# Forming half of the low parts of the first MLP product's weights with ScalarE and an accumulating DMA

## The chip, the core and the metric

The kernel runs on one core of one Trainium2 chip. The metric is the device time in microseconds of one execution. Each time is from a run of the whole program; the median of three runs is compared.

## The reference, cut to what matters

A decoder trunk of two layers on 256 tokens of width 2048, all in float32. Layer 0 has a mixer of a gated short convolution and differential attention, layer 1 has forgetting attention; each layer ends with a dense MLP whose hidden width is 8192:

```
def _sqrelu_mlp(h, w1, w2):
    return jnp.square(jax.nn.relu(h @ w1)) @ w2

for l in range(DEPTH):
    h = _rmsnorm(x, norm1_g[l])
    ...                                    # x = x + mixer(h)
    h = _rmsnorm(x, norm2_g[l])
    x = x + _sqrelu_mlp(h, mlp_w1[l], mlp_w2[l])
```

`mlp_w1` is 2 x 2048 x 8192 and `mlp_w2` 2 x 8192 x 2048. The weights of all products together are some 400 MB, read once, so the kernel is a stream of weights through 256 tokens.

## The kernel before

Every large product goes through `gemm(acts, w, c0)`, which makes 256 tokens x 512 columns in two PSUM tiles. To keep nearly float32 precision with matmuls on the narrower type float32r, each operand is split into a high part (the value rounded to float32r) and a low part (the rest, rounded too), and three products are added: high x high, high x low of the weights, low x high. The activations are split when they are made (`ActT`); the weights are split in `gemm`, as they arrive.

The weights come in raw tiles of 512 rows x 512 columns (1 MB), loaded by SP's DMA queue into a pool of three buffers (L135). Each raw tile is worked in two halves, h = 0 and 1. For a half tile ScalarE casts the raw values into the high part `wh` (L141), VectorE subtracts it from the raw values into the low part `wl` (L142), and TensorE does 12 matmuls: two token tiles, two k tiles, and the three products (L148 with `wh`, L149 with `wl`, L150 with `wh` and the low part of the activations). `wh` and `wl` have four buffers each. A buffer of `wh` is free again when the half tile that used it has gone through TensorE; a raw tile is free when both its halves are split.

`mlp` has four groups of hidden columns per layer. In each it does four products with w1 (L524), each followed by relu on ScalarE (L529), a multiplication on VectorE (L530) and transposes on TensorE (L514), and then four products with w2 (L538) over these 2048 hidden columns, added to the residual (L540). A product with w1 has 4 raw tiles, thus 8 half tiles; there are 2 x 16 such products.

The order of the instructions on each engine isn't that of the code. The kernel is written as a data flow over tile pools; when it is built, a scheduler puts each engine's instructions in an order of its own, by what it expects to be ready, and adds the waits. That order is then fixed: an engine's queue goes through it one by one, and an instruction that waits holds those behind it. The small work (attention, norms, transposes) is written as generators in `pending`, of which `step()` emits a stage after each half tile.

POOL has little to do: it makes masks at the start and adds the mask to the bias of layer 1's attention (L462).

Of the kernel before, what the change touches and what calls it, by code (L numbers as in the profile page):

```python
# [8 lines left out]
F32 = mybir.dt.float32  # L9
F32R = mybir.dt.float32r  # L10
# [16 lines left out]
def trunk_kernel(  # L27
# [20 lines left out]

    # ---------------------------------------------------------------- inputs
    xr = [resid.tile([P, 2, CW], F32, name=f"xr{n}") for n in range(NCH)]  # L50
# [9 lines left out]

    # per-channel vectors come as rows and are transposed: channels on partitions
    g1 = const.tile([P, 32], F32, name="g1")
# [10 lines left out]

    # ---------------------------------------------------------------- helpers
    pending = []

    def step():
        """Emit one more stage of the work that runs beside the large products."""
        while pending:
            try:  # L80
                next(pending[0])
                return True
            except StopIteration:
                pending.pop(0)
        return False
# [5 lines left out]
    def rsqrt(out_t, ss, inv_n, n):  # L91
        """out = (ss * inv_n + EPS) ** -0.5, one Newton step behind the tables."""
        v = small.tile([P, n], F32, name=f"rv{n}")
        nc.vector.tensor_scalar(v, ss, inv_n, EPS, ALU.mult, ALU.add)
        y = small.tile([P, n], F32, name=f"ry{n}")
        nc.scalar.activation(y, v, AF.Ln)
        nc.scalar.activation(y, y, AF.Exp, scale=-0.5)
        t = small.tile([P, n], F32, name=f"rt{n}")
        nc.vector.tensor_tensor(t, y, y, ALU.mult)
        nc.vector.scalar_tensor_tensor(t, t, -0.5, v, ALU.mult, ALU.mult)  # L100
        nc.vector.scalar_tensor_tensor(out_t, t, 1.5, y, ALU.add, ALU.mult)

    class ActT:
        """Transposed activations, four k tiles: high and low parts."""

# [6 lines left out]
        def split(self, sel, src, scalar, n):  # L112
            """hi/lo[sel] = parts of src * scalar; n: how many k tiles' worth it is."""
            hi, lo = self.hi[sel], self.lo[sel]
            if scalar is None:
                nc.scalar.copy(hi, src)  # L116
                nc.vector.tensor_tensor(lo, src, hi.bitcast(F32), ALU.subtract)  # L117
            else:
                nc.scalar.activation(hi, src, AF.Copy, scale=scalar)
                nc.vector.scalar_tensor_tensor(lo, src, scalar, hi.bitcast(F32), ALU.mult, ALU.subtract)  # L120
            self.left -= n

    def gemm(acts, w, c0, first=False):
        """acts @ w[:, c0:c0+512] -> two PSUM tiles (tokens x columns)."""
        acc = [accp.tile([P, CW], F32, name="acc") for _ in range(2)]
        total = 4 * len(acts)
        i = 0
        for ai, a in enumerate(acts):
            raw = wraw.tile([P, 4, CW], F32, name="raw")
            src = w[a.row:a.row + CW, c0:c0 + CW].rearrange("(k p) n -> p k n", p=P)  # L130
            if first and ai == 0:
                for h in range(2):
                    nc.sync.dma_start(raw[:, 2 * h:2 * h + 2, :], src[:, 2 * h:2 * h + 2, :])
            else:
                nc.sync.dma_start(raw, src)  # L135
            until(lambda: a.left <= 0)
            for h in range(2):
                wh = wspl.tile([P, 2, CW], F32R, name="wh")
                wl = wspl.tile([P, 2, CW], F32R, name="wl")
                rw = raw[:, 2 * h:2 * h + 2, :]  # L140
                nc.scalar.copy(wh, rw)  # L141
                nc.vector.tensor_tensor(wl, rw, wh.bitcast(F32), ALU.subtract)  # L142
                for t in range(2):
                    ts = slice(t * P, (t + 1) * P)
                    for j in range(2):
                        k = 2 * h + j
                        st, sp = i + j == 0, i + j == total - 1
                        nc.tensor.matmul(acc[t], a.hi[:, k, ts], wh[:, j, :], start=st, stop=False)  # L148
                        nc.tensor.matmul(acc[t], a.hi[:, k, ts], wl[:, j, :], start=False, stop=False)  # L149
                        nc.tensor.matmul(acc[t], a.lo[:, k, ts], wh[:, j, :], start=False, stop=sp)  # L150
                i += 2
                step()
        return acc

    class Norm:
        """Pre-RMSNorm of the residual: transposed x * g by chunk, and 1/rms by token."""

# [32 lines left out]
    def proj(nm, w, c0, name, first=False):  # L190
        """Rows of (norm(x) @ w)[:, c0:c0+512] in SBUF."""
        acc = gemm(nm.acts, w, c0, first)
        o = qkv.tile([P, 2, CW], F32, name=name)
        for t in range(2):
            nc.scalar.activation(o[:, t, :], acc[t], AF.Copy, scale=nm.r(t))
        return o

    # ---------------------------------------------------------------- setup
    # (emitted once the first loads are under way)
    lam_init = 0.8 - 0.6 * math.exp(-0.3 * 0)  # L200
# [10 lines left out]
    def setup():  # L211
# [14 lines left out]

        # causal masks: [first block | full block | diagonal block]
        nc.gpsimd.memset(mask, 0.0)
# [12 lines left out]
        nc.vector.tensor_copy(sv, ps[:, :NROW])  # L241
        # diff: q gain x k gain x scale; fox: the same; sub-norm gain x (1 - lambda_init)
        nc.vector.scalar_tensor_tensor(gains[:, 0:1], sv[:, 56:57], 64.0 ** -0.5, sv[:, 57:58], ALU.mult, ALU.mult)
        nc.vector.scalar_tensor_tensor(gains[:, 1:2], sv[:, 59:60], 128.0 ** -0.5, sv[:, 60:61], ALU.mult, ALU.mult)
        nc.vector.tensor_scalar(gains[:, 2:3], sv[:, 58:59], 1.0 - lam_init, None, ALU.mult)
        yield
        # -lambda on every partition
        lp = work.tile([P, 2, P], F32, name="y")[:, :, :64]
# [8 lines left out]
    def head_norm(tiles, hd):  # L257
        """RMS-normalise groups of hd columns of [P, 2, CW] tiles, in place, without gain."""
        g = CW // hd
# [33 lines left out]
    def prob_transposed(p):  # L293
        """[queries, (q0 k0 | q1 k0 | q1 k1)] -> the three blocks transposed."""
        ps = tpp.tile([P, CW], F32, name="tp")
        for b in range(3):
            nc.tensor.transpose(ps[:, b * P:(b + 1) * P], p[:, b * P:(b + 1) * P], ident)  # L297
        pT = work.tile([P, 3 * P], F32, name="pT")
        nc.scalar.copy(pT, ps[:, :3 * P])
        return pT  # L300

    # stages of four heads, staggered
    STAGES = [("T", 0), ("S", 0), ("T", 1), ("S", 1), ("P", 0), ("T", 2), ("A", 0), ("S", 2),
              ("P", 1), ("T", 3), ("A", 1), ("S", 3), ("P", 2), ("A", 2), ("P", 3), ("A", 3)]

    # ------------------------------------------------------- layer 0: mixers
    def diff_attention(q, k, v, a):
# [52 lines left out]
    def conv_mixer(c, u, b, half, a):  # L360
        """Gated causal convolution of 512 channels, channels on partitions."""
        for t in range(2):
# [24 lines left out]

    # ------------------------------------------------------- layer 1: mixer
    fc = const.tile([P, 2, 16], F32, name="fc")
    fcd = dram.tile([16, 2 * P], F32, name="fcd")  # L390

    def forget_gates(nm):
        """fc: cumulated log gates; fcd: their negative by head."""
        wv = gws[:, :KT * 32].rearrange("p (k n) -> p k n", n=32)
# [3 lines left out]
        yield  # L398
        # rows 0-15: high parts of w, rows 16-31: low parts; the other rows are not used
        acc = tpp.tile([P, CW], F32, name="tp")  # L400
# [26 lines left out]
        nc.vector.tensor_scalar(u, e, 1.0, None, ALU.add)  # L427
        # log1p(e) = ln(u) + (e - (u - 1)) / u
        nc.vector.scalar_tensor_tensor(d, u, -1.0, e, ALU.add, ALU.subtract)
# [67 lines left out]

    # ---------------------------------------------------------------- layers
    def out_proj(acts, w, nxt):
        """x += concat(acts) @ w; the last k block apart, as its input comes last."""  # L500
        for part in (acts[:-1], acts[-1:]):
            for n in range(NCH):
                acc = gemm(part, w, n * CW)
                for t in range(2):
                    nc.vector.tensor_tensor(xr[n][:, t, :], acc[t], xr[n][:, t, :], ALU.add)  # L505
                if len(part) == 1:
                    pending.append(nxt.chunk(n))

    def mlp(nm, l, nxt):
# [10 lines left out]
        for g in range(4):  # L520
            hT = []
            for n in range(4):
                c0 = (4 * g + n) * CW
                acc = gemm(nm.acts, mlp_w1[l], c0)  # L524
                a = ActT(c0)
                # relu(h)^2 without the 1/rms of each token, which follows behind w2
                r = [work.tile([P, CW], F32, name="junk") for _ in range(2)]
# [91 lines left out]
```

## Time and profile before

| | |
|---|---|
| runs | 2219.1, 2219.4, 2220.47 us; median 2219.4 |
| span of the profiled execution, first to last instruction | 2217.6 us (no time of its own is listed beside it; the runs lie 1.5 to 2.9 us above it) |
| TensorE matmul busy | 2207.0 us (100%) |
| VectorE busy | 1245.1 us (56%) |
| ScalarE busy | 1029.5 us (46%) |
| POOL busy | 13.7 us (1%) |
| DMA, mean | 186 GB/s, 412.02 MB |
| granted TensorE clock | 1.000, of 2.4 GHz |

An engine is busy while one of its instructions runs. Matmuls overlap: one has a duration of 390 ns, and they start about 227 ns apart (12 in 2.72 us). Idle time counts against an engine only where nothing else is in the way. "What ended it" names the instruction whose completion let the waiting one go.

### The profile page before, as it was taken

How to read it: one execution, taken by the hardware profiler on the slowest of the kernel's cores; microseconds unless marked ns; L12 is line 12 of the kernel's file. 1: busy time of each engine (PE TensorE's matmuls, PEld its weight loads, DVE VectorE, ACT ScalarE, POOL GpSimd, SP SyncE). 2: the span in 40 equal slices, each digit the busy share in tenths (PEclk: the TensorE clock that was granted, in tenths of full speed). 3: DMA queues.
4: the chain of work that ended last, by engine and by line, in shares of the span. 5: the costliest groups of instructions: out<-in, count | busy, mean ns of one | idle time of the engine just before them, and what ended most of it. 6: DMA issues, size and time to landing. Idle time of an engine off the chain costs nothing.

```text
span 2217.6 us, 25167 instructions
## 1 busy us (share of the span) xinstructions
PE 2207.0 (100%) x10100; PEld 1824.2 (82%) x10100; DVE 1245.1 (56%) x1480; ACT 1029.5 (46%) x1351; POOL 13.7 (1%) x17
## 2 busy tenths in 40 slices
PE   8999999999999999999999999999999999999999
PEld 7887888888888888888888888888888888888887
DVE  5666666655555555455556566666555555555554
ACT  6555444543443444344455555455434434443443
POOL 0000000000000000000000000000000000000000
PEclk9999999999999999999999999999999999999999
DMA  7555555555555555555555555555565555555564
GB/s 254 171 172 167 174 190 190 176 184 194 190 186 191 192 187 190 192 188 190 182 175 189 185 185 178 178 171 179 183 195 191 184 190 194 185 190 194 186 199 142
DMA packets 212470, 412.02 MB, mean 186 GB/s; under 512 B 9367, under 2 KB 13698, under 8 KB 212354
## 3 DMA queue, kind: packets, MB, share of 16 engines
q1 hardware_dynamic: 204496, 405.84, 56.2%
q10 hardware_dynamic: 7858, 4.58, 0.7%
q8 instruction: 79, 1.29, 0.2%
q14 instruction: 37, 0.30, 0.0%
HBM read 408.28 MB, written 2.11 MB: 185 GB/s over the span
## 4 chain that ended last, share of the span: by engine, by line
PE 99%; ACT 0%; DMA 0%; DVE 0%; SPq 0%; issue 0%
PE acc L148 32%; PE acc L150 32%; PE acc L149 32%; PE tp L514 1%; PE tp L169 1%; PE tp L285 0%; PE tp L297 0%; PE tp L473 0%; PE tp L493 0%; DMA xr<-in_x_dram 0%; PE tp L494 0%; PE tp L472 0%; PE tp L371 0%; PE tp L321 0%; PE tp L320 0%; PE tp L405 0%
## 5 line engine op out<-in xcount | busy, mean ns | idle before, releaser
L142 DVE TENSOR_TENSOR wl<-raw,wh 128x1024 fp32r<-128x1024 f32 x768 | 942.3, 1228 | 883.1 <-ACT wh L141 882.5
L141 ACT CAST wh<-raw 128x1024 fp32r<-128x1024 f32 x768 | 807.4, 1052 | 1081.3 <-PE acc L150 1039.2
L148 PE MATMUL acc<-wh,act_hi 128*128 128x512 f32 x3072 | 1219.2, 397 | 2.0 <-ACT wh L141 2.0
L150 PE MATMUL acc<-wh,act_lo 128*128 128x512 f32 x3072 | 1200.2, 391 | 0.0
L149 PE MATMUL acc<-wl,act_hi 128*128 128x512 f32 x3072 | 1198.5, 390 | 0.0
L150 PEld LDWEIGHTS acc<-wh,act_lo 128*128 128x128 f32 x3072 | 577.2, 188 | 122.8
L148 PEld LDWEIGHTS acc<-wh,act_hi 128*128 128x128 f32 x3072 | 577.8, 188 | 118.2 <-issue 2.7
L149 PEld LDWEIGHTS acc<-wl,act_hi 128*128 128x128 f32 x3072 | 578.3, 188 | 115.5 <-DVE wl L142 0.8
L529 ACT ACTIVATE junk<-acc 128x512 f32<-128x512 f32 x64 | 38.3, 598 | 34.1 <-PE acc L150 34.1
L530 DVE TENSOR_TENSOR junk<-acc,junk 128x512 f32<-128x512 f32 x64 | 44.0, 688 | 14.0 <-ACT junk L529 14.0
L117 DVE TENSOR_TENSOR act_lo<-tp,act_hi 128x512 fp32r<-128x512 f32 (+1 forms) x80 | 50.5, 631 | 0.8 <-ACT act_hi L116 0.7
L540 DVE SCALAR_TENSOR_TENSOR xr<-acc,r,xr 128x512 f32<-128x512 f32 x64 | 45.0, 744 | 7.8 <-PE acc L150 7.8
L116 ACT CAST act_hi<-tp 128x512 fp32r<-128x512 f32 (+1 forms) x80 | 42.9, 537 | 4.2 <-PE tp L494 4.2
L514 PEld LDWEIGHTS tp<-ident,junk 128*128 128x128 f32 x256 | 31.7, 139 | 8.2
L514 PE MATMUL tp<-ident,junk 128*128 128x128 f32 x256 | 38.3, 272 | 0.0
L478 DVE SCALAR_TENSOR_TENSOR s<-ob,fc,tp 128x128 f32<-128x128 f32 (+1 forms) x32 | 11.8, 411 | 20.4 <-PE tp L473 20.4
L169 PE MATMUL tp<-ident,xr 128*128 128x128 f32 x128 | 19.9, 282 | 2.0 <-DMA xr<-in_x_dram 2.0
L169 PEld LDWEIGHTS tp<-ident,xr 128*128 128x128 f32 x128 | 16.4, 145 | 6.0 <-DMA xr<-in_x_dram 2.1
L175 ACT ACTIVATE junk<-xr 128x512 f32<-128x512 f32 x32 | 19.9, 627 | 2.2 <-DMA xr<-in_x_dram 2.2
L505 DVE TENSOR_TENSOR xr<-acc,xr 128x512 f32<-128x512 f32 x32 | 20.8, 683 | 0.1
L462 POOL TENSOR_TENSOR ob<-ob,mask 128x512 f32<-128x512 f32 x8 | 12.2, 1535 | 1369.4 <-ACT wh L141 1168.1
L330 ACT ACTIVATE s<-s,mx 128x128 f32<-128x128 f32 (+1 forms) x32 | 14.2, 445 | 12.0 <-DVE mx L327 12.0
(138 smaller groups left out, 486.8 us busy)
## 6 DMA issues: line engine op xcount, KB each, us to landing
raw<-in_mlp_w_dram SPq DMA_DIRECT2D x256, 1024.0 KB, 5.1
raw<-in_fox_w_in_dram SPq DMA_DIRECT2D x48, 1024.0 KB, 5.1
raw<-in_hyb_w_in_dram SPq DMA_DIRECT2D x47, 1024.0 KB, 5.1
raw<-in_hyb_w_out_dram SPq DMA_DIRECT2D x16, 1024.0 KB, 5.1
raw<-in_fox_w_out_dram SPq DMA_DIRECT2D x16, 1024.0 KB, 5.1
ob<-fcd ACTq DMA_DIRECT2D x4, 512.0 KB, 3.7
xr<-in_x_dram SPq DMA_DIRECT2D x3, 512.0 KB, 7.2
raw<-in_hyb_w_in_dram SPq DMA_DIRECT2D x2, 512.0 KB, 5.4
```

The source lines that it names most:

```text
L116: nc.scalar.copy(hi, src)
L117: nc.vector.tensor_tensor(lo, src, hi.bitcast(F32), ALU.subtract)
L141: nc.scalar.copy(wh, rw)
L142: nc.vector.tensor_tensor(wl, rw, wh.bitcast(F32), ALU.subtract)
L148: nc.tensor.matmul(acc[t], a.hi[:, k, ts], wh[:, j, :], start=st, stop=False)
L149: nc.tensor.matmul(acc[t], a.hi[:, k, ts], wl[:, j, :], start=False, stop=False)
L150: nc.tensor.matmul(acc[t], a.lo[:, k, ts], wh[:, j, :], start=False, stop=sp)
L169: nc.tensor.transpose(ps[:, t * P:(t + 1) * P], xr[n][:, t, j * P:(j + 1) * P], ident)
L514: nc.tensor.transpose(ps[:, j * P:(j + 1) * P], r[t][:, j * P:(j + 1) * P], ident)
L529: nc.scalar.activation(r[t], acc[t], AF.Relu)
L530: nc.vector.tensor_tensor(r[t], acc[t], r[t], ALU.mult)
L540: nc.vector.scalar_tensor_tensor(xr[n][:, t, :], acc[t], r2[:, t:t + 1], xr[n][:, t, :], ALU.mult, ALU.add)
```

## The change

In `gemm` a new argument `dma_lo` is set for the products with w1 alone. There the second half of each raw tile (h = 1) gets its low part in another way: ScalarE writes the negated high part straight into `wl` (the raw values times -1, rounded to float32r), and then a DMA issued by POOL reads the same weights from HBM a second time and adds them to `wl` in place. ScalarE casts the high part as before. VectorE isn't used for that half. The first halves, and every other product, are formed as before. In all products `wh` now has three buffers and `wl` five, where both had four, so the same room is taken. The rest of the diff takes comments out.

```
-    def gemm(acts, w, c0, first=False):
+    def gemm(acts, w, c0, first=False, dma_lo=False):
...
-                wh = wspl.tile([P, 2, CW], F32R, name="wh")
-                wl = wspl.tile([P, 2, CW], F32R, name="wl")
+                wh = wspl.tile([P, 2, CW], F32R, name="wh", bufs=3)
+                wl = wspl.tile([P, 2, CW], F32R, name="wl", bufs=5)
                 rw = raw[:, 2 * h:2 * h + 2, :]
-                nc.scalar.copy(wh, rw)
-                nc.vector.tensor_tensor(wl, rw, wh.bitcast(F32), ALU.subtract)
+                if dma_lo and h == 1:
+
+                    nc.scalar.activation(wl, rw, AF.Copy, scale=-1.0)
+                    nc.gpsimd.dma_start(wl, src[:, 2 * h:2 * h + 2, :], accum_op=ALU.add)
+                    nc.scalar.copy(wh, rw)
+                else:
+                    nc.scalar.copy(wh, rw)
+                    nc.vector.tensor_tensor(wl, rw, wh.bitcast(F32), ALU.subtract)
...
-                acc = gemm(nm.acts, mlp_w1[l], c0)
+                acc = gemm(nm.acts, mlp_w1[l], c0, dma_lo=True)
```

## Rows read from the trace of the kernel before

**Rows 1.** The page's totals: busy us (share of the span) x instructions.

```profile
PE 2207.0 (100%) x10100; PEld 1824.2 (82%) x10100; DVE 1245.1 (56%) x1480; ACT 1029.5 (46%) x1351; POOL 13.7 (1%) x17
```

**Rows 2.** The page's chain that ended last, by engine and line.

```profile
PE 99%; ACT 0%; DMA 0%; DVE 0%; SPq 0%; issue 0%
...
PE acc L148 32%; PE acc L150 32%; PE acc L149 32%; PE tp L514 1%; PE tp L169 1%; PE tp L285 0%; PE tp L297 0%; PE tp L473 0%; PE tp L493 0%; DMA xr<-in_x_dram 0%; PE tp L494 0%; PE tp L472 0%; PE tp L371 0%; PE tp L321 0%; PE tp L320 0%; PE tp L405 0%
```

**Rows 3.** The page's costliest groups: busy us, mean ns | idle before, what ended it.

```profile
L142 DVE TENSOR_TENSOR wl<-raw,wh 128x1024 fp32r<-128x1024 f32 x768 | 942.3, 1228 | 883.1 <-ACT wh L141 882.5
L141 ACT CAST wh<-raw 128x1024 fp32r<-128x1024 f32 x768 | 807.4, 1052 | 1081.3 <-PE acc L150 1039.2
```

**Rows 4.** Waits, whole span: engine, line <- releaser: us in total, times, longest.

```profile
ACT wh L141 <- PE acc L150: 1039.2, 654, 3.6
DVE wl L142 <- ACT wh L141: 882.5, 688, 3.4
...
PEld acc L148 <- ACT wh L141: 2.4, 1, 2.4
...
PEld acc L149 <- DVE wl L142: 0.8, 1, 0.8
```

**Rows 5.** Timeline of ScalarE, first w1 products: start us, us, instruction [idle before].

```profile
407.44 1.05 ACT L141 CAST wh<-raw 128x1024 fp32r<-128x1024 f32 x1 [1.67 <-PE acc L150]
410.16 1.05 ACT L141 CAST wh<-raw 128x1024 fp32r<-128x1024 f32 x1 [1.67 <-PE acc L150]
412.88 1.05 ACT L141 CAST wh<-raw 128x1024 fp32r<-128x1024 f32 x1 [1.67 <-PE acc L150]
414.24 0.60 ACT L529 ACTIVATE junk<-acc 128x512 f32<-128x512 f32 x1 [0.30 <-PE acc L150]
415.60 0.60 ACT L529 ACTIVATE junk<-acc 128x512 f32<-128x512 f32 x1 [0.76 <-PE acc L150]
416.09 1.04 ACT L141 CAST wh<-raw 128x1024 fp32r<-128x1024 f32 x1
...
436.96 0.60 ACT L529 ACTIVATE junk<-acc 128x512 f32<-128x512 f32 x1 [0.31 <-PE acc L150]
```

**Rows 6.** Windows: start (DMA queue full), three w1 products, the following w2 products.

```profile
core 0: us, PE busy (x) PEld busy (x) DVE busy (x) ACT busy (x) POOL busy (x), PEclk, DMA share, GB/s
11.00:19.00 8.00, 8.00 (x37) 6.53 (x36) 4.14 (x7) 5.39 (x15) 0.00 (x0) 1.00 1.05 389
416.09:484.27 68.18, 68.18 (x314) 56.44 (x313) 36.89 (x36) 31.40 (x37) 0.00 (x0) 1.00 0.57 185
484.27:571.00 86.73, 86.73 (x388) 71.87 (x387) 44.70 (x41) 34.69 (x35) 0.00 (x0) 1.00 0.59 189
```

**Rows 7.** DMA issues (KB each, median us to landing), and L135's issue ns and landings.

```profile
raw<-in_mlp_w_dram SPq DMA_DIRECT2D x256, 1024.0 KB, 5.1
...
ob<-fcd ACTq DMA_DIRECT2D x4, 512.0 KB, 3.7
xr<-in_x_dram SPq DMA_DIRECT2D x3, 512.0 KB, 7.2
raw<-in_hyb_w_in_dram SPq DMA_DIRECT2D x2, 512.0 KB, 5.4
...
L135 SPq DMA_DIRECT2D raw<-in_mlp_w_dram x256: 367/368/368, 370.6 to 2189.0; - x128
...
DMA to landing us min/median/max: 4.9/5.1/8.5
```

**Rows 8.** POOL's longest line: duration ns min/median/max, first and last start us.

```profile
L462 POOL TENSOR_TENSOR ob<-ob,mask x8: 1286/1298/2357, 1170.3 to 1382.5; 128x512 f32<-128x512 f32 x8
```

**Rows 9.** Waits of the cast: 30 to 393 us, 1110 to 1500, 416.09 to 484.27.

```profile
ACT wh L141 <- PE acc L150: 131.3, 86, 2.1
...
ACT wh L141 <- PE acc L150: 144.2, 97, 3.6
...
ACT wh L141 <- PE acc L150: 33.6, 21, 1.7
```

**Rows 10.** Waits of SP's queue, whole span.

```profile
SPq L135 <- DVE wl L142: 1756.3, 335, 9.5
```

## The prediction

> **What bounds the kernel now.** I read the totals first, then the chain, then who waits for whom, then the first MLP product alone. TensorE is busy for 2207.0 of 2217.6 us [rows 1], and the chain that ended last is 99% TensorE, nearly all of it the three matmul lines of `gemm` [rows 2]. So there are 10.6 us in the whole span in which TensorE does nothing, and no edit that leaves its matmuls alone can win more than that. VectorE's subtraction is the costliest group off TensorE (768 at 1228 ns, [rows 3]), and it is mostly waiting itself: 882.5 us for ScalarE's cast, while the cast waits 1039.2 us for TensorE to give a buffer back. In the other direction TensorE's weight load waited once for VectorE's low part, 0.8 us, and once for the cast, 2.4 us [rows 4]. The producers are held back by buffers, not short of time.
>
> The stage that the change touches shows the same more sharply. In three products of the first MLP matrix (416.09 to 484.27 us) TensorE is busy for 68.18 of 68.18 us, VectorE for 36.89, ScalarE for 31.40, and the DMA engines have a share of 0.57 [rows 6], and the w2 products behind them show the same. There is no gap to close.
>
> The pace I need: casts start 2.72 us apart (407.44, 410.16, 412.88), which is one half tile, 12 matmuls. A product of 8 half tiles takes 22.72 us by its relu (414.24 to 436.96), the rest being transposes [rows 5]. Per 1 MB tile of w1 (a pair of half tiles) that is 22.72 / 4 = 5.68 us. The 2 x 16 products of w1 have 4 pairs each, so 128 pairs.
>
> **The change part by part.**
>
> *VectorE.* 128 subtractions at 1228 ns go, 157 us of its 1245.1 [rows 1, 3]. TensorE waited 0.8 us for that engine in the whole span, and not in the w1 stage, whose 68.18 us have no idle [rows 4, 6]. Worth 0.
>
> *ScalarE.* 128 negated casts are added. The form is the same as that of the cast (128x1024, scaled), so 1052 ns each [rows 3], 135 us. Per pair ScalarE goes from 31.40 / 12 = 2.62 us to 3.67 us of 5.68: 65% busy. It is covered by the 33.6 of 68.18 us in which the casts there wait for TensorE [rows 9], 2.8 us per pair. Cost 0, provided that it isn't held up by its own order (below).
>
> *Buffers.* The high parts have 3 buffers in place of 4, in every product of the kernel. Today a cast starts when the half tile four back ends (it shows as 1.67 us idle behind L150, [rows 5]), and cast and subtraction are through 1.05 + 1.23 = 2.3 us later. With three buffers the start is one half tile later: 2 x 2.72 - 2.3 = 3.1 us remain, where 5.9 did. In the mixers, where ScalarE has most else to do, the casts still wait for TensorE 86 times for 131.3 us and 97 times for 144.2 us, about 1.5 us each [rows 9]: ScalarE is ahead there, and a delay has to pass 3.1 us before it is felt. From 0 to a few us; I take 0.
>
> *POOL.* It does nothing in these stages (13.7 us in all, and its long instructions stand at 1170 us and later, [rows 1, 8]), and now issues 128 DMAs. No DMA from POOL is in this trace. From below, an issue on SP takes 0.37 us [rows 7]; from above I take POOL's longest instruction, 2.36 us [rows 8]. Either is less than 5.68 us per pair, so the queue keeps up; the length counts only as a part of the latency below. The additions of L462 are in layer 1's mixer, between the MLPs, and none of the new DMAs is queued next to them.
>
> *Raw tiles.* SP's reload waits for the last reader, which is the subtraction (335 waits, [rows 10]). For w1 it becomes the cast, so reloads go out some 1.2 us earlier. No gain, as nothing waits for raw.
>
> *DMA bandwidth.* This is what decides. Where the queue is never empty (11 to 19 us) the engines move 389 GB/s [rows 6]. A raw tile of 1.049 MB is then 2.70 us of all engines. The accumulate brings in 0.524 MB more per pair and has to read as much from the buffer that it adds to. No row shows such a transfer. Lower bound: it costs as much as a copy, 1.35 us, and the sum is 4.05 of 5.68 us (71%). If reading two operands costs two copies, it is 2.70, and the sum 5.40 (95%). The break-even is 5.68 - 2.70 = 2.98 us, or 2.2 copies. The upper bound from the nearest rows is the longest landing of 512 KB, 7.2 us [rows 7], all counted as engine time: 4.2 us too much per pair, 540 us in all. I take two copies, as the operands that have to be read are two, and the fixed part of a landing is no engine time (a 1 MB tile lands in 5.1 us where the engines need 2.70). That is hidden, with 5% to spare.
>
> The Trainium skill ("Collectives: The Full Stack", the section on the bandwidth ceiling and the fold count) says that an add inside the DMA engines costs no time for the adding but needs two source reads, and gives a measured ratio of 1.93 to a copy. By that the sum, an estimate, would be 2.70 + 1.93 x 1.35 = 5.3 us of 5.68, hidden too. No run here shows it yet.
>
> *Latency of the accumulate.* The low part of an odd half tile now takes: negated cast, POOL, DMA. From issue to landing the nearest rows are 3.7 us (512 KB from ScalarE's queue), 5.1 us (1 MB), and 8.5 us (the slowest 1 MB) [rows 7]; with up to 2.36 us on POOL, 3.7 to 10.9 us. How much may it take? If the negated cast stands in ScalarE's queue right behind the cast of the half tile before, which starts when the half tile four back has ended, it is through 2.1 us after that end and needed 3 x 2.72 us after it: 6.1 us. If it stands as early as the data allow, it starts when its raw tile has landed. That tile is asked for when the cast six half tiles back is done (three raw buffers), that is 1.05 us after the end of the one nine back, and lands 5.1 us later; with the cast that comes first, the negated one ends some 2.1 us after the end of the one seven back, six half tiles (16.3 us) before it is needed: 14.2 us, more than the upper bound. The five low-part buffers allow that: three go with the high parts, two are free for odd half tiles further on. I take the early order, since the program's queue orders show work placed when it is ready: the cast at 412.88 precedes the relu of the product that is still running, which comes in the code before it [rows 5]. Cost 0.
>
> *Sum.* 0 on TensorE's path: span 2217.6 us as before. The timed runs before had 2219.1 to 2220.47 us, median 2219.4, 1.8 us above the profiled span, so the forecast is 2219.5 us.
>
> **The rivals.**
>
> *The DMA engines become the bound in the w1 stages (slower).* Decides from 2.2 copies per accumulate. For it: 5% is no margin, two queues now interleave, and even at one copy the share rises from 0.57 to over 0.7. Against it: 1.5 MB per 5.68 us is 277 GB/s, well under the 389 seen [rows 6]. At three copies a pair needs 2.70 + 4.05 = 6.75 us, 1.07 too much, 137 us over 128 pairs: 2356 us. What three raw tiles hold at the start of each of the eight w1 stages would take off at most two pairs' excess in 16.
>
> *The accumulate lands too late (slower).* This is the late order with a latency above 6.1 us. A stall on each odd half tile moves the next start as well, so a pair loses half of the excess: at 8.5 us it is 1.2 us, 154 us in all, 2373 us; at 7 us 58 us, 2277 us. Against it: the five buffers and the order in the trace. For it: ScalarE's queue is in order, and a negated cast that waits for a late raw tile holds the casts behind it; it does harm from 3.1 us on.
>
> *TensorE runs faster.* It would need part of the 10.6 us, most of it outside the w1 stages, by another order of the work: up to 10 us, 2210 us. Nothing in the trace speaks for it; the step is 2.72 us with TensorE never waiting.
>
> **How the numbers follow.** Unchanged 0.49; the bandwidth bound 0.30; the late landing 0.17; faster 0.04. About 0.2%, 4.4 us, is what can be told from no change. The likeliest case alone is 2216 to 2224 us. The range goes to 2360 us, past three copies and most of the late landing; above it I leave 0.15 (dearer accumulates), below 2213 us 0.03. Chances: faster 0.04, within 0.2% 0.49, slower 0.47.
>
> **What would show it.** Right: in the w1 stages TensorE has no idle before L149's counterpart, products still 22.7 us apart, a DMA share of 0.70 to 0.95 there, VectorE about 157 us less busy, ScalarE about 135 us more. The bandwidth rival: a share near 1.0 there, raw tiles landing far later than 5.1 us, casts waiting for DMA. The late landing: TensorE waiting for the DMA into the low part while the share stays below 0.9. The forecast falls if a w1 product takes over 22.9 us.

## The result, and the profile after

The changed kernel takes 2276.34 us (median of 4 runs, 2275.16 to 2278.82) against 2219.53 us before: 1.0255 of the time, 95% interval 1.0243 to 1.0267, 57 us slower. The time lies in the stated range, but not where I put most weight: the forecast was no change, and what came is a rival, the accumulate that lands too late.

The page of the changed kernel, first the totals (to be held against [rows 1]), then DMA queues, the chain of [rows 2], and groups. In the changed file the three matmul lines are L154 to L156, the cast is L147 (L145 for a half whose low part comes by DMA), the subtraction L148, the negated cast L143, and POOL's DMA L144.

```profile
PE 2230.7 (98%) x10100; PEld 1822.2 (80%) x10100; DVE 1094.1 (48%) x1352; ACT 1151.9 (51%) x1479; POOL 167.0 (7%) x145
...
q1 hardware_dynamic: 204496, 405.84, 51.7%
q0 software_dynamic: 34816, 67.12, 18.0%
...
PE 82%; DMA 11%; issue 4%; ACT 1%; DVE 1%; POOL 0%; ACTq 0%; SPq 0%; POOLq 0%
PE acc L155 27%; PE acc L156 26%; PE acc L154 26%; DMA wl<-in_mlp_w_dram 11%; DVE wl L148 1%; ACT wh L147 1%; PE tp L291 0%; PE tp L175 0%; PE tp L520 0%; PE tp L303 0%; PE tp L479 0%; PE tp L499 0%; DMA xr<-in_x_dram 0%; PE tp L500 0%; PE tp L478 0%
...
L155 PEld LDWEIGHTS acc<-wl,act_hi 128*128 128x128 f32 x3072 | 579.0, 188 | 175.8 <-DMA wl<-in_mlp_w_dram 60.8
...
L144 POOL DMA_DIRECT2D wl<-in_mlp_w_dram x128 | 154.2, 1205 | 1643.9 <-DVE wl L148 936.1
...
L143 ACT ACTIVATE wl<-raw 128x1024 fp32r<-128x1024 f32 x128 | 135.2, 1056 | 0.0
...
raw<-in_mlp_w_dram SPq DMA_DIRECT2D x256, 1024.0 KB, 6.8
wl<-in_mlp_w_dram POOLq DMA_DIRECT2D x128, 512.0 KB, 6.0
```

VectorE is 151 us less busy, ScalarE 122 us more, as the change says. But the chain, which was 99% TensorE, now has 11% in the new DMA. That share is no price: 11% are 250 us, and 57 were lost, so the chain counts transfers that lay mostly beside matmuls. Where TensorE waits stands in the waits of the whole span (columns as in [rows 4]):

```profile
PEld acc L155 <- DMA wl<-in_mlp_w_dram: 60.8, 67, 3.3
...
PE acc L155 <- DMA wl<-in_mlp_w_dram: 35.2, 39, 2.8
```

The weight load ahead of the first matmul with `wl` waits 60.8 us, close to the whole loss (the spans are 59.5 us apart: 2277.1 and 2217.6). The same waits show in the matmul row as 35.2 us only, since part of each lies under the modelled end of the matmul before. By the matmuls' starts in the w1 products, the first matmuls with `wl` come 44.5 us later in sum than before, the matmuls right behind them about 7 us, and two stretches at half clock (below) cost 4. By the row, 67 of the 128 accumulates are late, by 0.9 us on average, 3.3 us at most.

The windows of a w1 stage and the w2 stage behind it (columns as in [rows 6]):

```profile
416.00:490.00 74.00, 71.42 (x321) 57.35 (x320) 24.35 (x26) 42.87 (x49) 13.36 (x12) 1.00 0.99 258
490.00:578.00 88.00, 88.00 (x394) 72.85 (x393) 44.88 (x42) 36.16 (x36) 1.20 (x1) 1.00 0.60 193
```

The w2 stage runs as before. In the w1 stage the DMA engines' share has gone from 0.57 to 0.99, which by itself would speak for the bandwidth rival; the experiments decide that.

One accumulate that comes late, in three timelines (start us, us, instruction [idle before <- releaser]): ScalarE, POOL and the weight loads.

```profile
418.51 1.05 ACT L147 CAST wh<-raw 128x1024 fp32r<-128x1024 f32 x1
419.45 1.06 ACT L143 ACTIVATE wl<-raw 128x1024 fp32r<-128x1024 f32 x1
420.74 1.05 ACT L145 CAST wh<-raw 128x1024 fp32r<-128x1024 f32 x1 [0.23 <-PE acc L156]
...
430.82 1.05 ACT L147 CAST wh<-raw 128x1024 fp32r<-128x1024 f32 x1 [2.63 <-PE acc L156]
431.78 1.05 ACT L143 ACTIVATE wl<-raw 128x1024 fp32r<-128x1024 f32 x1
```

```profile
420.81 1.20 POOL L144 DMA_DIRECT2D wl<-in_mlp_w_dram  x1 [4.68 <-DVE wl L148]
```

```profile
426.72 0.19 PEld L154 LDWEIGHTS acc<-wh,act_hi 128*128 128x128 f32 x1
427.95 0.19 PEld L155 LDWEIGHTS acc<-wl,act_hi 128*128 128x128 f32 x1 [1.04 <-DMA wl<-in_mlp_w_dram]
```

The negated cast at 419.45 stands right behind the cast of the half tile before it, which is the late order of the prediction. POOL starts 0.3 us after its end and takes 1.2 us; by the packet records the first packet leaves 1.9 us after POOL's start where nothing is in the way, the last ends 3.3 us later at the least, and the landing follows 0.3 to 0.4 us behind that. So 5.9 us from the negated cast's end to landing is the least; the median is 6.3 us, the mean 6.7. Here it was landed at 427.9, 7.4 us after the negated cast's end at 420.51; TensorE wanted it at 426.9.

### The profile page after: what moved, and what is told of

Read it like the earlier page. It is cut to its first block, busy times and chain, and to the rows that moved or that the text cites. A ratio compares the mean times of both kernels' runs of the same rounds, so it can differ in the third digit from the quotient of the medians.

```text
span 2277.1 us, 25670 instructions
## 1 busy us (share of the span) xinstructions
PE 2230.7 (98%) x10100; PEld 1822.2 (80%) x10100; DVE 1094.1 (48%) x1352; ACT 1151.9 (51%) x1479; POOL 167.0 (7%) x145
## 4 chain that ended last, share of the span: by engine, by line
PE 82%; DMA 11%; issue 4%; ACT 1%; DVE 1%; POOL 0%; ACTq 0%; SPq 0%; POOLq 0%
PE acc L155 27%; PE acc L156 26%; PE acc L154 26%; DMA wl<-in_mlp_w_dram 11%; DVE wl L148 1%; ACT wh L147 1%; PE tp L291 0%; PE tp L175 0%; PE tp L520 0%; PE tp L303 0%; PE tp L479 0%; PE tp L499 0%; DMA xr<-in_x_dram 0%; PE tp L500 0%; PE tp L478 0%
## 5 line engine op out<-in xcount | busy, mean ns | idle before, releaser
L148 DVE TENSOR_TENSOR wl<-raw,wh 128x1024 fp32r<-128x1024 f32 x640 | 784.5, 1227 | 964.8 <-ACT wh L147 964.0
L155 PE MATMUL acc<-wl,act_hi 128*128 128x512 f32 x3072 | 1206.9, 393 | 35.6 <-DMA wl<-in_mlp_w_dram 35.2
L154 PE MATMUL acc<-wh,act_hi 128*128 128x512 f32 x3072 | 1220.3, 397 | 2.0 <-ACT wh L147 2.0
L156 PE MATMUL acc<-wh,act_lo 128*128 128x512 f32 x3072 | 1202.0, 391 | 0.0
L147 ACT CAST wh<-raw 128x1024 fp32r<-128x1024 f32 x640 | 672.7, 1052 | 933.4 <-PE acc L156 853.5
L155 PEld LDWEIGHTS acc<-wl,act_hi 128*128 128x128 f32 x3072 | 579.0, 188 | 175.8 <-DMA wl<-in_mlp_w_dram 60.8
L156 PEld LDWEIGHTS acc<-wh,act_lo 128*128 128x128 f32 x3072 | 578.2, 188 | 121.3
L154 PEld LDWEIGHTS acc<-wh,act_hi 128*128 128x128 f32 x3072 | 578.7, 188 | 120.5 <-issue 2.7
L144 POOL DMA_DIRECT2D wl<-in_mlp_w_dram x128 | 154.2, 1205 | 1643.9 <-DVE wl L148 936.1
L145 ACT CAST wh<-raw 128x1024 fp32r<-128x1024 f32 x128 | 134.4, 1050 | 72.5 <-PE acc L156 72.5
L143 ACT ACTIVATE wl<-raw 128x1024 fp32r<-128x1024 f32 x128 | 135.2, 1056 | 0.0
```

Source lines behind the costliest of these rows:

```text
L143: nc.scalar.activation(wl, rw, AF.Copy, scale=-1.0)
L144: nc.gpsimd.dma_start(wl, src[:, 2 * h:2 * h + 2, :], accum_op=ALU.add)
```

## The experiments

Two theories. **Late landing:** the accumulate comes later than the room between its negated cast and its matmul allows. **Bandwidth:** the DMA engines can't carry the second read and the add at TensorE's pace. All are timed against the kernel before on the same chip.

### e1_bufs: the buffers alone

```
-                acc = gemm(nm.acts, mlp_w1[l], c0, dma_lo=True)
+                acc = gemm(nm.acts, mlp_w1[l], c0)
```

> The buffers alone: three for the high part and five for the low part in every product, all low parts formed by VectorE as before. The late-landing theory (TensorE waits for the accumulating DMA because its low part comes later than 6 us allow) and the bandwidth theory (the DMA engines can't carry the second read and the add) both expect the time of before, 2219.5 us within 3 us. A third theory, that three high-part buffers are too few, expects over 2230 us.

Measured 2220.29 us, ratio 1.0001 (0.9992 to 1.0011). Three buffers for the high part cost nothing when VectorE forms the low parts.

### e10_vecadd: ScalarE's extra casts without the DMA

```
-                    nc.gpsimd.dma_start(wl, src[:, 2 * h:2 * h + 2, :], accum_op=ALU.add)
+                    nc.vector.tensor_tensor(wl, rw, wl.bitcast(F32), ALU.add)
```

> The change with VectorE adding the weights to the negated high part in place of the DMA: ScalarE's 128 extra casts, its order and the buffers stay, no second read. All theories on the DMA expect the time of before, 2219 to 2222 us. If ScalarE's own extra work or its order holds TensorE up: over 2230 us.

Measured 2220.27 us, ratio 1.000 (0.999 to 1.001). With e1 this leaves the DMA and its issue on POOL as the cause.

### e2_early: the same DMAs, one half tile earlier

```
+            lows = [None, None]
+            if dma_lo:
+                lows[1] = wspl.tile([P, 2, CW], F32R, name="wl", bufs=5)
+                nc.scalar.activation(lows[1], raw[:, 2:4, :], AF.Copy, scale=-1.0)
+                nc.gpsimd.dma_start(lows[1], src[:, 2:4, :], accum_op=ALU.add)
             for h in range(2):
...              # casts of both halves, VectorE's subtraction for h = 0, matmuls
```

> The same 128 accumulating DMAs, but the negated high part of the odd half and its DMA stand in ScalarE's order ahead of the cast of the even half of the same tile, so they start one half tile (2.72 us) earlier. Late landing: the room grows from 6.1 to 8.8 us, landings of 5.6 to 8.7 us fit nearly all, and the time falls from 2276 to 2219 to 2230 us, with TensorE's waits for the low part's DMA under 10 us. Bandwidth: the engines have as much to move, the share in the w1 stages stays near 1.0 and the time at 2262 to 2280 us.

Measured 2226.89 us, ratio 1.0034 (1.0021 to 1.0047): 50 of the 57 us are back. The traffic is the same. The window of the w1 stage, the waits of the weight load and the DMA rows of this kernel (its matmul with `wl` is L156, its POOL DMA L141):

```profile
416.00:490.00 74.00, 74.00 (x341) 61.27 (x340) 27.15 (x29) 44.62 (x51) 12.03 (x10) 1.00 0.98 267
```

```profile
PEld acc L156 <- DMA wl<-in_mlp_w_dram: 6.2, 7, 1.8
```

```profile
raw<-in_mlp_w_dram SPq DMA_DIRECT2D x256, 1024.0 KB, 6.1
wl<-in_mlp_w_dram POOLq DMA_DIRECT2D x128, 512.0 KB, 8.9
```

At a share of 0.98 and 267 GB/s TensorE is busy for 74.00 of 74.00 us. The accumulate even takes longer here, 8.9 us from issue to landing in place of 6.0, and it hardly matters, because TensorE now wants it 11.5 us after the end of the negated cast in the median, 7.6 us at the least (worked out from the trace). The bandwidth theory falls as the explanation of the loss: what the share shows is engines that are nearly full, not too slow. That sharing them makes an accumulate longer is another matter, and comes up below.

### e6_alternate and e9_even: half as many accumulates, in two ways

```
-                if dma_lo and h == 1:
+                if dma_lo and h == 1 and ai % 2 == 1:    # e6: second and fourth raw tile
+                if dma_lo and h == 1 and ai % 2 == 0:    # e9: first and third raw tile
```

> The change in every second raw tile only, 64 accumulating DMAs. Bandwidth: a share near 0.8 in the w1 stages, nothing is over-asked, 2219 to 2222 us. Late landing: each accumulate has the same room as in the change, and no stall half a pair earlier that gives it more; with landings about 6.3 us after the negated cast against some 6.3 us of room, 0.2 to 0.9 us per accumulate, 2232 to 2277 us if the raw loads collide with it as often, 2222 to 2235 us if they don't.

> 64 accumulating DMAs again, now in the first and third raw tile of each product (half tiles 1 and 5) and none in the second and fourth. In the change's trace the stalls lie by half tile of the product: 7.2 us at 1, 26.5 at 3, 2.8 at 5, 9.8 at 7 (of which 2.2 us at 1 are there before the change too). If lateness goes by what stands ahead of the negated cast in ScalarE's order and of the DMA in the queues: a loss of 5 to 12 us, 2225 to 2232 us, against 2274 us with the same number in tiles two and four. If it goes by the number of accumulates: about as much as there, 2260 to 2280 us.

e6: 2274.25 us, ratio 1.0243 (1.0228 to 1.0259): with half the accumulates the loss is as large. e9: 2241.58 us, ratio 1.0101 (1.0085 to 1.0116). I had expected 2225 to 2232 for e9; it is dearer, but 33 us below e6 with the same number. The waits and windows, e6 first:

```profile
PEld acc L155 <- DMA wl<-in_mlp_w_dram: 56.6, 63, 3.4
```

```profile
416.00:490.00 74.00, 71.33 (x320) 57.17 (x319) 31.33 (x32) 37.68 (x43) 7.22 (x6) 1.00 0.78 217
```

```profile
PEld acc L155 <- DMA wl<-in_mlp_w_dram: 25.8, 41, 3.0
```

In e6, 63 of 64 accumulates are late, 0.9 us each, at a share of 0.78, with the engines a fifth idle. Worked out from the traces, the delay of each half tile's first matmul with `wl` (its start less that of the matmul before it, less the usual 0.23 us), summed over the 32 products of w1:

```
half tile of the product      0     1     2     3     4     5     6     7
before                      0.2   2.2   2.3   0.0   0.0   0.0   0.0   0.0
the change                  0.2   7.2   2.3  26.5   0.3   2.8   0.0   9.8
e6 (3 and 7 by DMA)         0.2   2.2   2.3  30.3   0.2   0.0   0.0   9.8
e9 (1 and 5 by DMA)         0.2   7.7   2.3   0.0   0.0   9.9   0.0   0.0
e2 (all odd, early)         0.2   2.9   2.3   0.0   0.0   0.0   0.0   3.6
```

Lateness goes by place, and in the trace of the change two places differ in kind (medians of 32 each). Half tile 7 has no margin: TensorE wants its low part 6.1 us after the negated cast's end, and it lands after 6.2. Half tile 3 has more room, 6.7 us, but its accumulate is longer: 4.8 us from first to last packet, against 3.6 to 3.7 at the other places. The relu of the product before comes into it: in the timeline above the cast at 418.51 begins 0.5 us after its buffer was free, since relu came first (the cast at 430.82 begins at once), and so the negated cast is late too, while L145, which TensorE releases, is not. SP's issue of the raw tile's reload, which follows L145, therefore ends 1.7 us after the negated cast in place of 2.1, and 262 raw packets start while the accumulate runs, in place of some 130. The two share the engines. That this spacing is the cause wasn't tested by itself; e3 below shows the same pattern.

A stall also makes room for the accumulates behind it: at half tile 5 TensorE wants the low part after 7.1 us in the change and after 6.1 in e9, where nothing is late at half tile 3. So half as many accumulates don't halve the loss, and half tile 5 costs more in e9 than in the change.

### e3_bufs44 and e7_poolraw: what stands ahead in the DMA engines

```
-                wh = wspl.tile([P, 2, CW], F32R, name="wh", bufs=3)
-                wl = wspl.tile([P, 2, CW], F32R, name="wl", bufs=5)
+                wh = wspl.tile([P, 2, CW], F32R, name="wh", bufs=4)
+                wl = wspl.tile([P, 2, CW], F32R, name="wl", bufs=4)
```

and in e7 besides

```
-                nc.sync.dma_start(raw, src)
+                (nc.gpsimd if dma_lo else nc.sync).dma_start(raw, src)
```

> The change with four buffers each for high and low parts, as before it. With four low-part buffers the negated cast can start when the half tile four back has ended; with four high-part buffers the cast ahead of it has been done a half tile earlier, so that the negated part is ready 1.05 us sooner. Late landing: 7.1 us of room, a loss of a quarter to a half of the 57 us, 2232 to 2250 us. Bandwidth: no change from 2276 us (2268 to 2284). If three buffers for the high part were the fault: 2220 us.

> The kernel with four buffers each (2329 us), and the raw tiles of w1 loaded by POOL's queue, where each stands behind the accumulating DMA issued before it. Collision theory (the four-buffer kernel got slower because its raw loads reached the DMA engines ahead of the accumulate, whose first packet then came 4 us after its issue in place of 1.9): the accumulate goes first again, is done 5.4 us after its issue against 7.3 us of room, 2219 to 2235 us. If order at the DMA engines isn't the cause: as slow as the four-buffer kernel, 2310 us or more.

e3: 2329.1 us, ratio 1.0491 (1.0475 to 1.0507). Both theories missed it: it is slower than the change, although its negated cast is ready about a us sooner. Its landings, from the line of POOL's DMA, against those of the change:

```profile
DMA to landing us min/median/max: 5.7/8.8/10.9
```

```profile
DMA to landing us min/median/max: 5.6/6.0/8.7
```

The first fence is e3, the second the change. With four high-part buffers the last cast of a raw tile is done sooner as well, so SP reloads the tile sooner: in e3 SP issues a reload at 432.54 us, 0.66 us after the accumulate's issue at 431.88. By the packet records the raw packets go first; the accumulate's first packet leaves at 435.88, 4.0 us after its issue in place of 1.9. In the change the same pair is 1.4 us apart, the accumulate is first, and it is the raw load that waits (3.2 us from issue to first packet), which nobody notices. One us of room was gained and 2.8 us of landing lost. By place: at half tiles 1 and 7 of e3 the reload's issue ends 1.3 us after the negated cast and the delays are 15.6 and 61.7 us; at 3 and 5 it ends 1.8 us after, and they are 5.1 and 5.6 us. Some 15 of the 109 us lost in e3 are eleven stretches of 3.4 us at half the clock.

e7: 2273.77 us, ratio 1.0247 (1.0231 to 1.0262). Putting the raw loads behind the accumulates in POOL's own queue gave back 55 of e3's 109 us, not all as the collision theory had it: its accumulates still took 7.6 us in the median. So e7 agrees with the order at the engines as a part of e3's loss; that it is all of it isn't shown, as e7 also changes the load path (raw tiles 9.5 us to landing by POOL's queue, 5.1 by SP's).

### e5_copy and e8_all: the price of the add

```
-                    nc.gpsimd.dma_start(wl, src[:, 2 * h:2 * h + 2, :], accum_op=ALU.add)
+                    nc.gpsimd.dma_start(wl, src[:, 2 * h:2 * h + 2, :])     # e5
```

e8 has e2's early form for both halves.

> The change with a plain copy in place of the adding DMA, from the same queue, at the same place, into the same buffer; the low part of the odd half is then the weights themselves and not the rest (this is left out). A row of 2 KB cost 176 ns with the add and 84 ns as a copy by SP; as a copy it should cost 84 here too. Both theories expect the loss to go, 2219 to 2225 us, since the DMA is some 1.5 us shorter and the engines have 1.35 us less to do. If the fixed part (POOL and the start of the queue, 0.3 + 1.9 us) were enough to make it late: over 2250 us.

> The low parts of both halves by accumulating DMAs, all negated casts ahead of the high casts, VectorE out of the first MLP product. Bandwidth must now bind: 2.70 us for the raw tile and 2 x 2.8 to 3.2 us for the adds are 8.3 to 9.1 us per pair against 5.68, so 2.6 to 3.4 us x 128 = 335 to 435 us, 2555 to 2655 us with a share of 1.0. If accumulates overlap with loads at little cost to the engines: under 2400 us.

e5: 2226.02 us, ratio 1.0032 (1.0019 to 1.0044). A 2 KB packet has a median of 99 ns as a copy (I expected 84), against 176 to 178 ns with the add and 84 ns for the raw loads; landing takes 4.2 us in the median, 1.8 us less, and the loss is gone but for 6 us. The fixed part alone isn't too late. Of the 1.8 us, 1.25 lie in the packets and 0.5 ahead of the first one, which leaves 1.42 us after POOL's start (POOL's instruction takes 0.71 us as a copy, 1.20 with the add). The add is dearer in both, and which part would be enough isn't shown.

e8: 2517.87 us, ratio 1.1343 (1.1326 to 1.136), somewhat under what I expected. Its window, with a share over 1:

```profile
416.00:490.00 74.00, 57.99 (x238) 42.13 (x239) 5.54 (x8) 38.91 (x44) 20.99 (x18) 1.00 1.10 262
```

Here bandwidth does bind: 298 us over 128 pairs are 2.33 us, so a pair takes 5.68 + 2.33 = 8.0 us; less the raw tile's 2.70 us each accumulate has 2.65 us, 1.97 times its copy's 1.35. This takes the engines as full throughout and all of the loss as theirs, so it is an estimate.

### e4_spare: the traffic without the wait

```
-                wl = wspl.tile([P, 2, CW], F32R, name="wl", bufs=5)
+                wl = wspl.tile([P, 2, CW], F32R, name="wl", bufs=3)
...              # the change's own branch goes, and for all halves:
                 if dma_lo and h == 1:
+                    wx = wspl.tile([P, 2, CW], F32R, name="wx", bufs=2)
+                    nc.scalar.activation(wx, rw, AF.Copy, scale=-1.0)
+                    nc.gpsimd.dma_start(wx, src[:, 2 * h:2 * h + 2, :], accum_op=ALU.add)
+                nc.scalar.copy(wh, rw)
+                nc.vector.tensor_tensor(wl, rw, wh.bitcast(F32), ALU.subtract)
```

> All low parts come from VectorE as before, and the negated parts with their 128 accumulating DMAs go to spare buffers (two) that no matmul reads; three buffers each for high and low parts. The traffic and ScalarE's work of the change are there, TensorE's wait for them isn't. Late landing: 2219 to 2225 us, no wait of TensorE. Bandwidth: raw tiles come late or the spare buffers aren't given back in time, ScalarE is held up, 2255 to 2280 us.

Measured 2232.78 us, ratio 1.0061 (1.0045 to 1.0078), between the two. TensorE waits little, and now for VectorE, which waits for ScalarE; the negated casts wait 271.4 us:

```profile
ACT wx L143 <- DMA raw<-in_mlp_w_dram: 271.4, 122, 4.4
...
PEld acc L153 <- DVE wl L146: 13.8, 23, 1.1
```

The row is right to name the raw load and not the accumulate two before, whose spare buffer is needed: that one had landed 2.0 us or more before each negated cast began, while the cast began 0.1 to 0.2 us after its raw tile's landing in all 46 cases where the trace gives that landing. So the negated cast here stands so early in ScalarE's queue that it waits for its raw tile, and the casts behind it wait with it, which the prediction names among its rivals. The 13 us are an upper bound for what the traffic costs by itself, and that order is a part of them.

## Why the prediction was right or wrong

*VectorE, ScalarE, buffers: right.* Each was put at 0, and e1 and e10 measure 0 within 0.1%. *Raw tiles: right only as far as it goes.* TensorE doesn't wait for them, but when their reloads go out isn't without effect, as half tile 3 and e3 show: there they meet the accumulate.

*DMA bandwidth: right.* Two copies per accumulate were taken, 5.40 us of 5.68. The packets show 176 / 84 = 2.1 against SP's load (1.8 against POOL's own copy), e8 gives some 1.97, and e2 runs TensorE without idle at a share of 0.98. The Trainium skill ("Collectives: The Full Stack", the section on the bandwidth ceiling and the fold count) has a measured 1.93 for two source reads against one, there of two collectives; these runs lie on both sides of it. The bandwidth rival, to which I gave 0.30, was not the cause, though at twice the traffic (e8) it is. The sign that I had named to tell the two apart, a share below 0.9 for the late landing, was badly chosen: it was 0.99, as two copies per accumulate (95%) would have it under either theory.

*Latency of the accumulate: wrong, and it is the step that decided.* Its numbers held: I had 6.1 us of room in the late order and 3.7 to 10.9 us from negated cast to landing, and the trace has 6.1 to 7.1 us of room by place (medians) and 5.9 us at best, 6.3 in the median to landing. What failed is the choice between the orders. I took the early one because a cast precedes a relu in the order before. That showed only that casts run ahead of a relu which can't start yet; it didn't show that a negated cast would run ahead of the cast that stands before it in the code. The changed kernel's order keeps the code's: cast, negated cast, cast. The five low-part buffers, which allow the early order, don't bring it about. e2, which writes the negated cast ahead of the even half's cast, gets 50 us back. So the cost that was put at 0 measured 57 us.

*The rival's price.* For 7 us of latency the prediction had 58 us, and 57 came, but not in that way, so the agreement is luck: the average latency is 6.7 us, and the loss isn't spread over 128 pairs but sits in the late ones, more than half of it in half tile 3. A margin of a few tenths of a us decides, and a raw load that runs beside the accumulate uses it up. The prediction counted the meeting of the two queues with the bandwidth rival, not as a longer landing.

*A cost that I hadn't priced: the clock.* Before, TensorE had its full clock to the last matmul. In the change's longest wait (3.27 us, ended at 2091.86) the granted clock falls to half, at 2091.1:

```profile
2079.00:2091.00 12.00, 10.01 (x44) 7.79 (x42) 3.95 (x4) 6.11 (x6) 2.41 (x2) 1.00 0.97 240
2091.00:2098.00 7.00, 6.14 (x15) 4.80 (x16) 0.00 (x0) 0.99 (x2) 0.00 (x0) 0.51 0.93 272
2098.00:2110.00 12.00, 12.00 (x54) 9.93 (x53) 3.84 (x5) 7.30 (x10) 2.41 (x2) 1.00 0.73 170
```

For nearly 7 us the level is 1.2 GHz, and matmuls start 0.43 us apart in place of 0.23. Together with one more such stretch of 3.4 us, behind a wait of 2.7 us, it is about 4 us of the 57; the mean over the span is 0.997.

*Left open:* the 7 us that e2 still loses. Its waits for the DMA are 6.2 us in 7 places; why these few land late is open. No version beats the kernel before, and none could by more than the 10.6 us that TensorE stood idle there.

## What to carry to other kernels

Taking work off an engine that isn't the bound gains nothing, and moving it to a DMA puts a long latency where a short instruction was: before such a move, count the room from the last input to the first use in the engine's actual order, and write the early order out, since free buffers alone don't make the program run ahead. A DMA share near 1 is no proof that bandwidth binds; hold the traffic and move the start (e2), or halve the traffic and leave the start (e6), and see which one moves the time. A buffer more can make things slower when it lets a load reach the DMA engines ahead of the transfer that is needed first (e3).

## What the runs showed of the hardware

- A DMA that adds into SBUF took 176 to 178 ns per 2 KB packet in the median, a copy from the same queue 99 ns (e5), a load by SP's queue 84 ns.
- From POOL's start to the first packet 1.92 us with the add (POOL busy for 1.20), 1.42 us as a copy (POOL busy for 0.71, e5); from the start of SP's issue 1.04 us, medians where nothing was in the way.
- With two transfers near each other, the first one held the other's first packet back: raw loads left 3.2 us after their issue behind an accumulate, accumulates 4.0 us after theirs behind raw loads. Once both ran, they shared the engines: the accumulate of half tile 3 took 4.8 us from first to last packet, where 3.6 to 3.7 were usual.
